# Hymba-style encoder trunk on one core: GLA scores of both directions by turns on row halves, output products in two column halves

## The chip, the cores and the metric

The kernel runs on one core of a Trainium2 chip. The metric is the device time of one execution in microseconds; the time before is the median of three runs.

## What is computed

Two layers of a bidirectional encoder over 1024 tokens of width 1024. Each layer adds to x an output projection of three head groups that share one input projection. The change touches two of them: the gated linear attention (GLA, 4 heads, key width 64, value width 96, one scan per direction) and the cross-attention into 256 memory tokens (4 heads of width 64). Cut to these:

```python
def _gla_chunked(q, k, v, g):
    b = jnp.cumsum(g, axis=-2)
    q_e = q * jnp.exp(b)
    k_e = k * jnp.exp(-b)
    a = jnp.where(incl, jnp.einsum('bhncd,bhnsd->bhncs', q_e, k_e), 0.0)
    o_intra = jnp.einsum('bhncs,bhnsv->bhncv', a, v)
    ...
    return o_intra + jnp.einsum('bhncd,bhndv->bhncv', q_e, s_prev)
...
    scores = jnp.einsum('bthd,bmhd->bhtm', q3, mk) * (XA_DH ** -0.5)
    p = jax.nn.softmax(scores, axis=-1)
    o3 = jnp.einsum('bhtm,bmhd->bthd', p, mv)
```

The GLA runs once forwards and once backwards and both are summed. The third group, a gated delta rule, is a serial recurrence over 16 chunks in both directions.

## The kernel before

Tokens stand in 8 tiles of 128. In each layer a first part normalises and transposes x and makes the dense projections (matmuls of 128x128 by 512 columns, in three passes of split fp32). Then `phase_mix` runs the serial chain of the delta rule (`chain`, matmuls that the trace shows as cp<-S,wq, R<-vn,kend, cp<-vn,qkt, pt<-kv,Mb and pt<-Mb,ke) and fills the time between its steps with other work: after each block of the chain, `filler` hands out units until their nominal nanoseconds reach a budget of 1200. What is left when the chain ends follows without it.

One kind of filler is the mixer (`mixes`), one tile of tokens after the other in the order `ORD`. For a tile it steps two generators:

- `xa_tile` has five units: softmax scores of two heads (x<-kh,xq and x<-kl,xq: four matmuls; then VectorE takes the maximum and ScalarE two exponentials); scores of the other two; transposes of the first two heads' exponentials (ident,pe), copied to pT; transposes of the other two; the value product (mv,pT: 128x128 by 64 columns, 4 heads by 2 halves of the memory).
- `gla_tile` has three units before: scores of one direction (x<-gqk or ga<-gqk: 64 rows, one row half of the array, by 128 columns, 4 heads), masked into As by a VectorE copy; scores of the other direction on the other row half, masked into the same As; then GpSimd multiplies As by `twice`, and TensorE forms the output product (gS,gqk and gv,As: 128x128 by 96 columns, 4 heads each).

Every mixer unit counts 700 nominal ns. All matmuls keep their program order, so a matmul that waits holds up all behind it, those of the chain as well. Other engines' instructions are placed by a scheduler. Four tiles of a layer are mixed while the chain runs and four afterwards, between the matmuls of the output projection (mm<-wo,oh and mm<-wo,ol; `out_tile`).

While the chain runs, PSUM tags ga, gb and tr stand for the tag x, which has two banks; gb becomes mm (two banks) in the middle of it. After the chain ga, gb and tr have two banks each. The tiles gqk, gv, gS (loads of the GLA) and xq have one buffer each, so a load waits until the tile's last reader is done.

An fp32 matmul is two records in the trace: the four score matmuls of a direction show as x8.

Of the kernel before, what the change touches and what calls it, by code (L numbers as in the profile page):

```python
# [17 lines left out]
P = 128  # L18
# [3 lines left out]
NT = 8  # L22
# [20 lines left out]
DC0 = 0  # L43
CUT = 30
MIX0 = 5
MIXN = 18
GAP0 = 4
GU = (4, 6)
TRN = 4
# [6 lines left out]
ORD = (4, 3, 5, 2, 6, 1, 7, 0)  # L56


class Kern:
# [768 lines left out]
    def filler(self, l, xin, xout, GP, closeGP):  # L828
# [28 lines left out]
        done = units = 0  # L857
        busy = True
        while busy:
            if units < 24:  # L860
                next(mixer)
                units += 1
                yield 700
            while busy and done < units * left // MIXN:

                if self.h0_done:
                    next(wout, None)
                busy = next(self.dense, None) is not None
                done += 1
                if busy:  # L870
                    yield 1290
# [2 lines left out]
        self.alias["gb"] = "mm"  # L874
        while self.wo[0][KT - 1] is None:
            next(wout)
            if units < 24:
                next(mixer)
                units += 1
                yield 700  # L880
        self.closeW()
        self.open_out(l)
        for _ in range(units, 24):
            next(wout, None)
            next(mixer)
            yield 700
# [10 lines left out]
        for i in range(NT + 1):  # L897
            g = None
            if i:
                t = ORD[i - 1]  # L900
                if i < NT:
                    x = self.OB.tile([P, D], F32, tag="xr", name="xr", bufs=1)
                else:
                    x = self.OX.tile([P, D], F32, tag="big", name="xr", bufs=2)
# [5 lines left out]
                for u, _ in enumerate(self.out_tile(self.OB, t, x, xout, then)):  # L910
# [6 lines left out]
                    if g is None and ready(i):  # L917
                        g = self.gate_tile(self.OG, ORD[i])
# [4 lines left out]
            while i < NT and g is None:  # L923
                if ready(i):
                    g = self.gate_tile(self.OG, ORD[i])
# [24 lines left out]
    def open_mix(self):  # L950
        self.OX, self.closeOX = self.pool("OX", side=self.sb)
        self.xa_setup(self.OX)
        self.gla_setup(self.OX)
        self.om, self.loaded = {}, {}
        self.mixed = 0
        self.mix_load(ORD[0])

    def open_out(self, l):
        self.OG, self.closeOG = self.pool("OG", side=self.sb)
# [3 lines left out]
            self.fw = self.OB.tile([P, D], F32, name="fw")  # L963
            self.nc.sync.dma_start(self.fw, self.a["final_norm_w"].to_broadcast([P, D]))

    def mix_load(self, t):
        self.loaded[t] = self.xa_load(self.OX, t), self.gla_load(self.OX, t)

    def mixes(self):

        for i, t in enumerate(ORD):
            o = self.om[t] = self.OX.tile([P, 640], F32, tag="o", name="o", bufs=3)
            xl, gl = self.loaded.pop(t)
            x = self.xa_tile(self.OX, xl, o[:, 384:640])
            g = self.gla_tile(self.OX, gl, o[:, 0:384])
            for j, u in enumerate((x, g, x, g, x, x, g, x)):
                next(u, None)
                if j == 6 and i + 1 < NT:
                    self.mix_load(ORD[i + 1])
                if j == 7:  # L980
                    self.mixed = i + 1
                yield

# [372 lines left out]
    def gla_tile(self, G, loaded, o):  # L1356

        qk, vt, S = loaded
        A = G.tile([P, 4, P], F32, tag="As", name="As", bufs=2)
        for d in range(2):  # L1360
            pa = self.ps("ga", [P, 4, P])
            r = slice(d * 64, d * 64 + 64)
            for h in range(4):
                self.mat(pa[:, h, :], qk[r, h, 1, :], qk[r, h, 0, :], start=True, stop=True)
            self.nc.vector.copy_predicated(A, self.mask[d].unsqueeze(1).to_broadcast([P, 4, P]), pa)  # L1365
            yield
        self.ptt(A, A, self.twice.unsqueeze(1).to_broadcast([P, 4, P]), ALU.mult)
        po = self.ps("gb", [P, 4, HD])
        for h in range(4):
            self.mat(po[:, h, :], qk[:, h, 0, :], S[:, h, :], start=True, stop=False)  # L1370
            self.mat(po[:, h, :], A[:, h, :], vt[:, h, :], start=False, stop=True)
        self.act(o.rearrange("p (h d) -> p h d", h=4), po)
        yield

# [74 lines left out]
    def xa_tile(self, XP, xq, o):  # L1449

        nc = self.nc
        mv = self.mv
        sc = 64 ** -0.5
        pe = XP.tile([P, 4, MEM], F32, tag="big", name="pe", bufs=2)
        sm = XP.tile([P, 4], F32, tag="xsm", name="xsm", bufs=2)
        mx = XP.tile([P, 4], F32, tag="xmx", name="xmx", bufs=2)

        for hh in range(2):
            psc = self.ps("ga", [P, 2, MEM])
            hs = slice(hh * 2, hh * 2 + 2)  # L1460
            for pr in range(2):
                i = hh * 2 + pr
                self.mat(psc[:, pr, :], xq[:, i, :], self.kh[:, i, :], start=True, stop=False)
                self.mat(psc[:, pr, :], xq[:, i, :], self.kl[:, i, :], start=False, stop=True)
            nc.vector.tensor_reduce(mx[:, hs], psc, op=ALU.max, axis=AX.X)
            nc.vector.tensor_scalar(mx[:, hs], mx[:, hs], -sc, None, op0=ALU.mult)
            for pr in range(2):
                i = hh * 2 + pr
                self.act(pe[:, i, :], psc[:, pr, :], AF.Exp, scale=sc, bias=mx[:, i:i + 1],
                         accum_out=sm[:, i:i + 1])  # L1470
            yield
        nc.vector.reciprocal(sm, sm)
        pT = XP.tile([P, 4, 2, P], F32, tag="big", name="pT", bufs=2)
        for g in range(2):
            ps = self.ps("gb", [P, 4, P])
            for j in range(4):
                i, m = g * 2 + j // 2, j % 2
                self.tpose(ps[:, j, :], pe[:, i, m * 128:m * 128 + 128], self.ident)
            self.evac(pT[:, g * 2:g * 2 + 2].rearrange("p a b c -> p (a b) c"), ps)
            yield  # L1480
        po = self.ps("gb", [P, 4, 64])
        for i in range(4):
            hd = (i % 2) * 2 + i // 2
            for m in range(2):
                self.mat(po[:, i, :], pT[:, i, m, :], mv[:, m, hd * 64:hd * 64 + 64],
                         start=m == 0, stop=m == 1)

        self.tt(o.rearrange("p (q h d) -> p h q d", q=2, h=2),
                po.rearrange("p (h q) d -> p h q d", h=2),
                sm.rearrange("p (h q) -> p h q", h=2).unsqueeze(3).to_broadcast([P, 2, 2, 64]), ALU.mult)  # L1490
        yield
# [164 lines left out]
```

## Time and profile before

| | us |
|---|---|
| runs | 1433.19, 1434.46 (median), 1443.61 |
| profiled execution, its own time | 1429.31 |
| its span, first to last instruction | 1427.6 |
| TensorE busy in the span | 1298.7 |
| VectorE, ScalarE, GpSimd busy | 841.6, 633.7, 566.9 |

Busy time of TensorE counts each matmul until its modelled end, so neighbours overlap; what a matmul costs the engine is read from start to start. In the first layer the mixer's matmuls lie from 495 to 675 us, in the second from 1202 to 1392 us; the chain ends near 590 and 1303 us.

### The profile page before, as it was taken

The numbers are of one execution on the slowest core, as the hardware profiler recorded it, in microseconds if no ns is written. First come the engines' busy times: TensorE is split into PE (matmuls) and PEld (weight loads), VectorE is DVE, ScalarE is ACT, GpSimd is POOL, SyncE is SP. The second block draws the span as 40 slices with busy tenths as digits, with TensorE's granted clock in tenths as the row PEclk, the third lists the DMA queues.
The fourth block names the chain that finished last, engine by engine and source line by source line (L and its number), as shares of the span: only waits on it lengthen the run. The fifth ranks groups of instructions, "written<-read, shape, count | busy, mean of one in ns | idle before, by whom it ended". The sixth has DMA issues, their size and how long they took to land. (4 is left out here: it accounts for less than half of the span.)

```text
span 1427.6 us, 23239 instructions
## 1 busy us (share of the span) xinstructions
PE 1298.7 (91%) x8970; PEld 1089.7 (76%) x8970; DVE 841.6 (59%) x1267; ACT 633.7 (44%) x1269; POOL 566.9 (40%) x597
## 2 busy tenths in 40 slices
PE   6998799898899989999899978987978999999998
PEld 5986588676687778888798757865857877888886
DVE  5346864595678455445362677536947874545553
ACT  5344654254655443223252455513355554433332
POOL 3035435494434345212310544354953344442111
PEclk9999999998999999999999999998989999989999
DMA  7251325733787654253543413266346875622432
GB/s 224 64 117 45 103 61 158 250 115 97 198 225 202 186 179 120 78 156 114 186 158 79 98 30 104 84 179 217 89 122 184 242 220 157 211 86 78 155 100 104
DMA packets 247855, 198.94 MB, mean 139 GB/s; under 512 B 68032, under 2 KB 215936, under 8 KB 247744
## 3 DMA queue, kind: packets, MB, share of 16 engines
q1 hardware_dynamic: 245584, 189.59, 46.1%
q10 hardware_dynamic: 2016, 7.34, 1.3%
q8 instruction: 71, 1.16, 0.3%
q0 software_dynamic: 144, 0.52, 0.1%
q14 instruction: 40, 0.33, 0.1%
HBM read 138.82 MB, written 58.59 MB: 138 GB/s over the span
## 5 line engine op out<-in xcount | busy, mean ns | idle before, releaser
L97 PE MATMUL mm<-Hh,wh 128*128 128x512 f32 x736 | 311.5, 423 | 36.5 <-ACT acc L83 19.6
L97 PE MATMUL mm<-Hh,wl 128*128 128x512 f32 x736 | 295.2, 401 | 0.0
L97 PE MATMUL mm<-Hl,wh 128*128 128x512 f32 x736 | 295.2, 401 | 0.0
L89 POOL TENSOR_TENSOR wl<-wr,wh 128x1024 fp32r<-128x1024 f32 x46 | 119.1, 2588 | 205.2 <-ACT wh L83 182.8
L97 PEld LDWEIGHTS mm<-Hh,wh 128*128 128x128 f32 x736 | 143.1, 194 | 71.0 <-ACT acc L83 22.9
L534 DVE SCALAR_TENSOR_TENSOR acc<-pad,convw,acc 128x1024 f32<-128x1024 f32 x72 | 141.5, 1966 | 67.9 <-ACT acc L83 53.1
L97 PE MATMUL mm<-wo,oh 128*128 128x512 f32 x512 | 167.5, 408 | 0.4 <-ACT oh L83 0.4
L97 PEld LDWEIGHTS mm<-Hh,wl 128*128 128x128 f32 x736 | 143.2, 195 | 32.2
L97 PEld LDWEIGHTS mm<-Hl,wh 128*128 128x128 f32 x736 | 144.1, 196 | 25.9
L97 PEld LDWEIGHTS mm<-wo,oh 128*128 128x128 f32 x512 | 89.8, 189 | 18.6 <-ACT oh L83 0.8
L97 PE MATMUL mm<-wo,ol 128*128 128x512 f32 x256 | 101.2, 395 | 0.6 <-POOL ol L89 0.6
L89 POOL TENSOR_TENSOR acc<-acc,pad 128x1024 f32<-128x1024 f32 x18 | 45.6, 2532 | 109.8 <-ACT pad L83 109.8
L89 POOL TENSOR_TENSOR S<-S,dec 96x384 f32<-96x384 f32 x56 | 52.6, 939 | 84.8 <-DVE S L86 54.8
L83 ACT ACTIVATE wh<-wr 128x1024 fp32r<-128x1024 f32 x46 | 48.4, 1053 | 75.7 <-PE mm L97 60.7
L89 POOL TENSOR_TENSOR ol<-z,oh 128x512 fp32r<-128x512 f32 x32 | 40.9, 1281 | 93.6 <-ACT oh L83 89.7
L97 PEld LDWEIGHTS cp<-S,wq 96*128 96x128 f32 x480 | 64.9, 204 | 16.3 <-ACT vn L83 4.9
L97 PE MATMUL cp<-S,wq 96*128 96x96 f32 x480 | 68.3, 289 | 9.3 <-ACT vn L83 3.6
L89 POOL TENSOR_TENSOR sp<-sp,sg 128x512 f32<-128x512 f32 x32 | 44.0, 1376 | 44.1 <-ACT sg L83 33.3
L97 PEld LDWEIGHTS mm<-wo,ol 128*128 128x128 f32 x256 | 48.1, 188 | 12.5 <-POOL ol L89 1.1
L97 PEld LDWEIGHTS R<-vn,kend 64*96 64x96 f32 x448 | 43.3, 165 | 16.9 <-issue 8.1
L89 POOL TENSOR_TENSOR row<-row,qT 96x1024 f32<-96x1024 f32 x16 | 38.0, 2385 | 45.2 <-DMA row<-row_d 29.4
L89 POOL TENSOR_TENSOR As<-As,twice 128x512 f32<-128x512 f32 x16 | 20.4, 1276 | 86.9 <-DVE As L1365 46.7
(313 smaller groups left out, 2746.3 us busy)
## 6 DMA issues: line engine op xcount, KB each, us to landing
wr<-in_w_in_dram SPq DMA_DIRECT2D x46, 512.0 KB, 4.1
kv<-kv_d SPq DMA_DIRECT2D x32, 384.0 KB, 3.9
zT<-sp SPq DMA_DIRECT2D x32, 256.0 KB, 3.0
ge_d<-qe SPq DMA_DIRECT2D x32, 256.0 KB, 3.7
wor<-in_w_out_dram SPq DMA_DIRECT2D x16, 512.0 KB, 4.3
gqk<-ge_d SPq DMA_DIRECT2D x16, 512.0 KB, 4.1
z<-zT SPq DMA_DIRECT2D x16, 512.0 KB, 4.5
row<-row_d SPq DMA_DIRECT2D x16, 384.0 KB, 6.6
```

Source lines behind the costliest of these rows:

```text
L83: return self.nc.scalar.activation(out, in_, func, **kw)
L89: return self.nc.gpsimd.tensor_tensor(out, a, b, op=op)
L97: return self.pin(self.nc.tensor.matmul(*args, **kw))
L534: nc.vector.scalar_tensor_tensor(acc, pad[:, j:j + T], self.convw[:, f, j:j + 1], acc, op0=ALU.mult, op1=ALU.add)
```

## The change

The GLA scores of both directions become one unit: each has a PSUM bank of its own, and the matmuls alternate between the directions, which means between row halves of the array. The output product and the value product write the same results, but each matmul is split into two with 64 stationary columns, for PSUM partitions 0 to 63 and 64 to 127, by turns. A tile then has seven units instead of eight, in a new order: both softmax scores, both transposes, GLA scores, value product, GLA output. The load of xq is issued after the second unit, that of the GLA's tiles after the last. The counts that spread the first three tiles over the dense work change with it (24 to 21 units, 18 to 16).

```diff
-MIXN = 18
+MIXU = 21
+MIXN = 16
...
-            if units < 24:
+            if units < MIXU:
...
-            xl, gl = self.loaded.pop(t)
-            x = self.xa_tile(self.OX, xl, o[:, 384:640])
-            g = self.gla_tile(self.OX, gl, o[:, 0:384])
-            for j, u in enumerate((x, g, x, g, x, x, g, x)):
+            x = self.xa_tile(self.OX, self.loaded["x"], o[:, 384:640])
+            g = self.gla_tile(self.OX, self.loaded["g"], o[:, 0:384])
+            for j, u in enumerate((x, x, x, x, g, x, g)):
                 next(u, None)
-                if j == 6 and i + 1 < NT:
-                    self.mix_load(ORD[i + 1])
-                if j == 7:
+                if j == 1 and i + 1 < NT:
+                    self.loaded["x"] = self.xa_load(self.OX, ORD[i + 1])
+                if j == 6:
+                    if i + 1 < NT:
+                        self.loaded["g"] = self.gla_load(self.OX, ORD[i + 1])
                     self.mixed = i + 1
...
+        pa = [self.ps("ga", [P, 4, P]) for _ in range(2)]
+
+        for h in range(4):
+            for d in range(2):
+                r = slice(d * 64, d * 64 + 64)
+                self.mat(pa[d][:, h, :], qk[r, h, 1, :], qk[r, h, 0, :], start=True, stop=True)
         for d in range(2):
-            pa = self.ps("ga", [P, 4, P])
-            r = slice(d * 64, d * 64 + 64)
-            for h in range(4):
-                self.mat(pa[:, h, :], qk[r, h, 1, :], qk[r, h, 0, :], start=True, stop=True)
-            self.nc.vector.copy_predicated(A, self.mask[d].unsqueeze(1).to_broadcast([P, 4, P]), pa)
-            yield
+            self.nc.vector.copy_predicated(A, self.mask[d].unsqueeze(1).to_broadcast([P, 4, P]), pa[d])
         self.ptt(A, A, self.twice.unsqueeze(1).to_broadcast([P, 4, P]), ALU.mult)
+        yield
         po = self.ps("gb", [P, 4, HD])
+
+        cs = [slice(c * 64, c * 64 + 64) for c in range(2)]
         for h in range(4):
-            self.mat(po[:, h, :], qk[:, h, 0, :], S[:, h, :], start=True, stop=False)
-            self.mat(po[:, h, :], A[:, h, :], vt[:, h, :], start=False, stop=True)
+            for c in cs:
+                self.mat(po[c, h, :], qk[:, h, 0, c], S[:, h, :], start=True, stop=False)
+            for c in cs:
+                self.mat(po[c, h, :], A[:, h, c], vt[:, h, :], start=False, stop=True)
...
-                self.mat(po[:, i, :], pT[:, i, m, :], mv[:, m, hd * 64:hd * 64 + 64],
-                         start=m == 0, stop=m == 1)
+
+                for c in (slice(0, 64), slice(64, 128)):
+                    self.mat(po[c, i, :], pT[:, i, m, c], mv[:, m, hd * 64:hd * 64 + 64],
+                             start=m == 0, stop=m == 1)
```

What this does to TensorE's queue is shown at three places. In these rows a count is of matmuls (two records each). First, the end of the second tile of the first layer, during the chain. Before:

```order
L97 MATMUL cp<-S_4713,wq 128x96 x4
L97 MATMUL pt<-Mb_3166,ke 96x128 x4
L97 MATMUL x<-gqk 128x128 x4
L100 MATMUL mm<-ident,pe 128x128 x8
L97 MATMUL mm<-gS,gqk 128x96
L97 MATMUL mm<-gv,As 128x96
```

And with the change:

```order
L98 MATMUL cp<-S_4734,wq 128x96 x4
L98 MATMUL pt<-Mb_3166,ke 96x128 x4
L98 MATMUL x<-gqk 128x128 x8
L98 MATMUL mm<-mv,pT 64x64 x16
L98 MATMUL mm<-gS,gqk 64x96 x2
L98 MATMUL mm<-gv,As 64x96 x2
```

Between the last scores and the first gv,As stand now the value product's 16 half matmuls, where eight transposes stood; and only the second direction's scores came so late before. Second, the fourth tile of the first layer, with the change:

```order
L98 MATMUL x<-kh,xq 128x256
L98 MATMUL x<-kl,xq 128x256
L98 MATMUL x<-kh,xq 128x256
L98 MATMUL x<-kl,xq 128x256
L101 MATMUL mm<-ident,pe 128x128 x8
L98 MATMUL mm<-wo_4698,oh 128x512 x2
```

Before, these scores were followed by other work:

```order
L97 MATMUL x<-kh,xq 128x256
L97 MATMUL x<-kl,xq 128x256
L97 MATMUL x<-kh,xq 128x256
L97 MATMUL x<-kl,xq 128x256
L97 MATMUL R<-vn,kend 96x96 x4
L97 MATMUL x<-gqk 128x128 x4
L97 MATMUL mm<-wo_4677,oh 128x512 x2
```

So the transposes of the second pair of heads now come directly behind that pair's scores. Third, after the chain, where a tile's units lie between output matmuls; with the change:

```order
L98 MATMUL ga<-gqk 128x128 x8
L101 MATMUL tr<-ident,o 128x128 x3
L101 MATMUL tr<-ident,oa_3161 128x128
L98 MATMUL mm<-wo_5049,oh 128x512 x2
L98 MATMUL mm<-wo_5049,ol 128x512
L98 MATMUL mm<-wo_5076,oh 128x512 x2
L98 MATMUL mm<-wo_5076,ol 128x512
L98 MATMUL gb<-mv,pT 64x64 x16
L98 MATMUL mm<-wo_5093,oh 128x512 x2
```

Here the scores, the value product and the output product keep six output matmuls (two steps of wo) between each other, as before.

## Rows read from the trace of the kernel before

**Rows 1.** The page: span, and busy time of the engines.
```profile
span 1427.6 us, 23239 instructions
...
PE 1298.7 (91%) x8970; PEld 1089.7 (76%) x8970; DVE 841.6 (59%) x1267; ACT 633.7 (44%) x1269; POOL 566.9 (40%) x597
```

**Rows 2.** Windows: length, busy us (x instructions) of PE, PEld, DVE, ACT, POOL, granted clock, DMA.
```profile
494.90:580.00 85.10, 80.15 (x674) 71.60 (x672) 47.65 (x90) 36.61 (x89) 43.48 (x45) 0.98 0.47 138
...
592.00:672.00 80.00, 80.00 (x482) 67.83 (x481) 42.21 (x88) 25.76 (x69) 16.50 (x13) 1.00 0.41 124
...
1242.30:1259.30 17.00, 17.00 (x88) 16.16 (x89) 8.59 (x18) 5.65 (x16) 4.89 (x5) 0.50 0.29 89
1214.00:1300.00 86.00, 81.52 (x633) 73.55 (x628) 42.99 (x81) 33.72 (x78) 34.46 (x36) 0.90 0.44 133
```

**Rows 3.** Timeline of PE after the chain: start us, length us, instruction, records.
```profile
594.72 0.40 PE L97 MATMUL mm<-wo,ol 128*128 128x512 f32 x1
595.05 1.16 PE L97 MATMUL ga<-gqk 64*128 64x128 f32 x8
596.13 0.73 PE L97 MATMUL mm<-wo,oh 128*128 128x512 f32 x2
...
606.32 0.35 PE L97 MATMUL gb<-gS,gqk 128*128 128x96 f32 x2
...
608.07 0.38 PE L100 MATMUL tr<-ident,oa 128*128 128x128 f32 x2
...
609.91 1.89 PE L97 MATMUL gb<-mv,pT 128*128 128x64 f32 x16
611.61 0.71 PE L97 MATMUL mm<-wo,oh 128*128 128x512 f32 x2
```

**Rows 4.** Timeline of PE, one of 16 groups of column-half matmuls, 64 wide.
```profile
241.81 0.40 PE L97 MATMUL mm<-Hl,wh 128*128 128x512 f32 x1
242.04 0.40 PE L97 MATMUL mm<-Hh,wl 128*128 128x512 f32 x1
242.37 0.34 PE L97 MATMUL cp<-kT 96*64 96x64 f32 x4
...
243.45 0.50 PE L97 MATMUL mm<-Hh,wh 128*128 128x512 f32 x1
```

**Rows 5.** Timeline of PE, one of 16 groups of column-half matmuls, 96 wide.
```profile
413.79 0.88 PE L97 MATMUL x<-gv,kt 128*64 128x96 f32 x16
414.60 0.50 PE L97 MATMUL mm<-Hh,wh 128*128 128x512 f32 x1
```

**Rows 6.** Timeline of PE, GLA scores and R on different row halves.
```profile
521.89 0.32 PE L97 MATMUL R<-vn,kend 64*96 64x96 f32 x1
521.99 0.27 PE L97 MATMUL x<-gqk 64*128 64x128 f32 x1
522.05 0.24 PE L97 MATMUL R<-vn,kend 64*96 64x96 f32 x1
522.11 0.27 PE L97 MATMUL x<-gqk 64*128 64x128 f32 x1
```

**Rows 7.** Groups by form, DVE, ACT and POOL: busy us, mean ns, idle before.
```profile
L1465 DVE TENSOR_REDUCE xmx<-x 128x2 f32<-128x512 f32 x16 | 11.0, 690 | 8.5 <-PE x L97 8.3
L1365 DVE COPY_PREDICATED As<-mB,x 128x512 f32<-128x512 int32 x8 | 5.9, 733 | 1.6 <-PE x L97 1.6
...
L83 ACT ACTIVATE pe<-x,xmx 128x256 f32<-128x256 f32 x32 | 14.9, 469 | 25.5 <-DVE xmx L1466 25.5
L83 ACT ACTIVATE pT<-x 128x512 f32<-128x512 f32 x6 | 3.5, 591 | 1.7 <-PE x L100 1.6
...
L89 POOL TENSOR_TENSOR As<-As,twice 128x512 f32<-128x512 f32 x16 | 20.4, 1276 | 86.9 <-DVE As L1365 46.7 <-DVE xsm L1472 40.2
```

**Rows 8.** Groups of PE from 494 to 580 us with the longest idle time before them.
```profile
L97 PE MATMUL cp<-S,wq 96*128 96x96 f32 x104 | 14.1, 278 | 1.9 <-ACT vn L83 1.8
...
L100 PE MATMUL x<-ident,pe 128*128 128x128 f32 x16 | 3.0, 320 | 1.4 <-ACT pe L83 1.4
```

More of the change, by code (lines that the diff above doesn't have):

```diff
@@ L876, in filler @@
             next(wout)
-            if units < 24:
+            if units < MIXU:
                 next(mixer)
@@ L882, in filler @@
         self.open_out(l)
-        for _ in range(units, 24):
+        for _ in range(units, MIXU):
             next(wout, None)
@@ L955, in open_mix @@
         self.mixed = 0
-        self.mix_load(ORD[0])
+        self.loaded["x"], self.loaded["g"] = self.xa_load(self.OX, ORD[0]), self.gla_load(self.OX, ORD[0])
     def open_out(self, l):
@@ L964, in open_out @@
             self.nc.sync.dma_start(self.fw, self.a["final_norm_w"].to_broadcast([P, D]))
-    def mix_load(self, t):
-        self.loaded[t] = self.xa_load(self.OX, t), self.gla_load(self.OX, t)
     def mixes(self):
```

## The prediction

> **What bounds the kernel now.** I read the page first: TensorE is busy for 1298.7 of 1427.6 us, the next engine for 841.6 [rows 1]. Then the windows, since the change lives in two stretches of each layer. After the chain, from 592 to 672 us, TensorE is busy for all 80.00 us at full clock, VectorE for 42.21, ScalarE for 25.76 [rows 2]: there every nanosecond taken from its queue should come off the time. While the chain runs and tiles are mixed, from 494.9 to 580 us, it is busy for 80.15 of 85.10 us, so 4.95 us are waits; the same stretch of the second layer has 81.52 of 86.00, 4.48 us of waits [rows 2]. The busiest other engine there has 47.65 us. So TensorE's queue, with its waits, is the time, and I count in starts along that queue.
>
> One more thing is to be seen in the windows: the granted clock. From 1242.3 to 1259.3 us it is 0.50 (1.2 instead of 2.4 GHz) with TensorE busy throughout, and 0.90 over the whole second stretch; in the first layer it is 0.98 over the stretch [rows 2], which is 0.02 x 85.1 x 2 = 3.4 us at half clock.
>
> **The change part by part.** A lone matmul record of the dense kind follows the one before after 0.23 us (241.81 to 242.04) [rows 4]; what a unit adds to such a stream is its cost.
>
> *Scores.* Eight records of one direction start at 595.05, the next output matmul at 596.13: 1.08 us, and the way in took 0.33 instead of 0.23 us [rows 3]. So 1.18 us a unit, two units a tile, 2.36 us. Can two row halves run at once with full columns? No row shows this very unit, but one place does nearly: scores and R on the other row half ran into each other. Scores start at 521.99 and 522.11, 0.12 us apart, no more than the 1.08 / 8 = 0.135 of an undisturbed unit, with records of R at 521.89 and 522.05 between them [rows 6]. Neither stream gave way. So 16 records by turns should take what eight take: 1.18 us. Bounds: 0 saved if the halves don't overlap and only one way in and out (0.2 us) goes, 1.18 if they do. I take 1.18, by rows 6.
>
> *Value product.* Now 16 records from 609.91 to 611.61, 1.70 us [rows 3]. That is 0.106 us each for 64 columns, while the 96-wide ones of the output product take 1.75 / 16 = 0.109; the width is not what is paid. After: 32 records of 64 stationary columns, 64 wide, on two column halves. The rows of the kT group are just that (32 records, 96 rows instead of 128): from 242.37 to 243.45 1.08 us, and 0.10 more on the way in (242.04 to 242.37 instead of 0.23) [rows 4]: 1.18 us. Saved 0.52.
>
> *Output product.* Now from 606.32 to 608.07, 1.75 us [rows 3]. After: 32 records, 96 wide, in column halves. Sixteen such records take from 413.79 to 414.60, 0.81 us with the way out [rows 5]. Twice that, 1.62, is the most; the least is 0.81 and eight pairs more at 0.08 (0.81 less some 0.2 for the ends, over eight pairs), 1.45. I take 1.5, and 0.1 for the way in as above: 1.6. Saved 0.15 (0.03 to 0.2).
>
> Sum for a tile: 1.18 + 0.52 + 0.15 = 1.85 us; 16 tiles, 29.6 us. Half of it, 14.8 us, lies after the chain, where the order shows six output matmuls (6 x 0.23 = 1.4 us) between any two units, and VectorE and ScalarE have half their time free. There I expect no new wait: As is ready 2 x 0.73 + 1.28 = 2.7 us, with handing over some 3.0, after the scores [rows 7], and six output matmuls (1.4), the value product (1.2) and another six (1.4) stand before it is read.
>
> *Waits during the chain.* Here the new order takes cover away. All of what follows is for four tiles of a layer, in the order shown.
> First tile: both banks of x are needed by the scores at once, and the second is freed by the copy of the second transposes (0.59 us, some 0.8 with handing over) [rows 7], which stand directly before: 0.8 us.
> Second tile: As is ready some 3.0 us after the scores, and only the value product (1.18) stands between: 1.9 us, where the one-direction unit waited less, since one masked copy was long done.
> Third tile: transposes of the first heads need a maximum (0.69), a scaling, two exponentials of 0.47 with the read of their sums [rows 7], some 2.2 us; a chain step and the second scores cover about 1.4: 0.8 us. Then As again with one chain step more before it: 0.9 us.
> Fourth tile: the second transposes directly behind their scores: 2.2 less the first transposes' 0.45, 1.75 us.
> Together 6.1 us a layer. What goes: the wait of 1.4 us on exponentials [rows 8] and the rest that hangs on the GLA's late loads, some 3 us of the 4.95 together; the chain's own 1.9 us on vn [rows 8] stays. Queued behind each of these waits are the chain's next steps, so they count in full. Net 3.1 us a layer, 6.2 in all; bounds: 0, if the chain would wait there anyway, and 12, if nothing of the old waits goes.
>
> *Clock.* 17.0 and 3.4 us at half clock now cost up to 10.2 us. The trace can't show what the new order does to them. Bounds: all of it is won (10.2), or as much comes again (-10). The value products and scores become denser, which should shorten the long spell, but the waits of some 2 us are longer than any now. I take half of what stands: 5 us won.
> The Trainium skill, in "TensorE: Matmul & The Clock Gate", Part 1, has the clock fall after idle time and rise after busy time; in the long spell the trace shows it staying low while TensorE counts as busy throughout [rows 2]. By that rule alone the long spell would not last, and its 8 us would be no term at all.
>
> The rest costs nothing: the loads of xq and of the GLA tiles come earlier against their readers (four units of cover instead of two), and SP's queue holds the same transfers; VectorE and ScalarE do the same operations. Two banks for the scores cost what is counted above.
>
> Sum against the profiled execution: 1429.3 - 29.6 + 6.2 - 5 = 1400.9. The runs' median is 5.2 us above that execution, so I forecast **1406 us**. A measurement of this kernel can tell about 1% from no change.
>
> **Rivals.**
> *A: the chain's stretch gives nothing.* Waits and lost cover eat the 14.8 us of the eight tiles there, the clock stays as it is: 1434.5 - 14.8 = 1420. For it: every unit there now hangs on another engine's answer; against it: the first tile's 1.4 us wait goes for sure.
> *B: the clock stays up* and the waits hide in the chain's own: 1434.5 - 29.6 - 8 = 1397. For it: the spell in the second layer has no counterpart at the same place of the first [rows 2], so a small shift can remove it.
> *C: row halves take turns.* The change then doesn't do what it says for the scores; 1.0 us a tile, 16 us, are lost of the gain, and the clock's share with it: 1434.5 - 13.6 + 6.2 = 1427. Against it stand rows 6.
> *D: column halves don't overlap, slower.* Each product then has 32 records one after another. A half record alone costs between 0.05, half of what a whole one does now, and 0.106 [rows 3]; at 0.08, 32 are 2.6 us instead of 1.70 and 1.75, so 1.75 us more a tile against the scores' 1.18 less: 0.57 x 16 = 9 more, with the waits 1434.5 + 9 + 6 = 1450. It decides from 0.13 us a pair on ((5.81 - 1.18 - 0.6) over 32 pairs). Rows 4 and 5 are against it (1.08 / 16 = 0.07 and 0.81 / 8 = 0.10 a pair).
> The Trainium skill has such a rule in "TensorE: Matmul & The Clock Gate", Part 3 (The mechanism): weight loads overlap running matmuls only when the row group differs, which column halves don't; the trace disagrees, with 16 records in 0.81 us [rows 5].
> *E: half clock spreads* over the chain's stretches, behind the new waits. From some 50 us more at 1.2 GHz than now the gain is gone; 80 us more give 1434.5 - 23.4 + 40 = 1451. Against it: after the chain the clock is 1.00 throughout [rows 2], so it could only be the chain's two stretches of 86 us.
>
> **How the numbers follow.** Forecast (1400 to 1413) 0.52, B 0.2, A 0.15, C 0.05, D 0.03, E 0.05. The range runs from 1392, B with all 10 us of the clock and no wait added (1434.5 - 29.6 - 10 = 1395) less 3 for the units' own bounds, to 1424, above A; C, D and E lie outside. Faster by over 1% (under 1420) takes the forecast, B and 0.1 of A: 0.82; within 1%: the rest of A, C and 0.02 of E, 0.12; slower: D and the rest of E, 0.06.
>
> **What would show it.** After the chain the time between two tiles' GLA scores falls by 1.85 us; the scores' 16 records take about as long as eight did, the value product 1.2 us, the output product 1.6. TensorE's rows during the chain show idle time on As, pe and pT, about 8 us a layer. I am wrong if score records of both directions don't start in pairs, if those idle times pass 12 us a layer, or if the windows show more half clock than the 20 us of now.

## The result and the profile after

The changed kernel takes 1425.0 us (median), the kernel before 1434.2: ratio 0.9935, 95% interval 0.991 to 0.996. The forecast was 1406.0 with a range of 1392 to 1424. So the change is worth some 9 us, not 28, and the time lies just outside the range, on the side of too little gain.

The page after (span and busy time, as [rows 1]):

```profile
span 1427.6 us, 24281 instructions
...
PE 1289.7 (90%) x9482; PEld 1068.1 (75%) x9482; DVE 843.9 (59%) x1267; ACT 631.4 (44%) x1269; POOL 568.6 (40%) x597
```

The two profiled executions happen to have the same span (before's was 4.9 us faster than its median, after's 4.4 us slower), so where the time went must be read inside. Only the stretch from the first softmax-score matmul to the last output matmul of each layer has changed. These are the windows over it, before and after (columns as in [rows 2]), with the two longest half-clock spells of after beneath:

```profile
494.91:708.48 213.57, 207.58 (x1388) 177.47 (x1387) 103.47 (x200) 71.53 (x177) 72.78 (x89) 0.99 0.45 136
1201.73:1420.28 218.55, 213.49 (x1387) 183.62 (x1387) 111.03 (x206) 80.20 (x199) 65.65 (x62) 0.96 0.39 123
```

```profile
495.43:708.61 213.18, 200.05 (x1643) 165.65 (x1643) 105.48 (x200) 70.14 (x176) 73.37 (x86) 0.96 0.45 135
546.40:560.00 13.60, 13.60 (x76) 12.37 (x72) 3.05 (x5) 3.80 (x8) 6.61 (x8) 0.50 0.49 131
1206.07:1420.23 214.16, 202.13 (x1643) 166.21 (x1643) 111.06 (x206) 78.88 (x199) 63.80 (x60) 0.95 0.41 125
1256.30:1273.40 17.10, 16.34 (x102) 15.05 (x103) 3.11 (x7) 3.90 (x8) 7.31 (x9) 0.50 0.37 105
```

What to see: TensorE's busy time falls from 207.58 + 213.49 = 421.07 to 402.18 us, 18.9 us less; but the length falls only from 432.12 to 427.34, because its idle time (length less busy) rises from 11.05 to 25.16 us. And the granted clock falls from 0.99 to 0.96 in the first layer and from 0.96 to 0.95 in the second: the spells at half clock in these stretches add up to 20.5 us before and 37.5 us after. Outside the stretches the two executions differ too, with 102.0 us at half clock before and 125.6 after; how much of it stands there differs from one execution to the next (101.5 in e8, the same kernel again). So the stretches account for 4.8 us between two single executions, and the rest of the 9 us between the medians has no account here.

Cut at the last matmul of the chain, the same stretches read, before and then after:

```profile
494.91:590.25 95.34, 90.39 (x743) 80.14 (x742) 50.94 (x95) 37.71 (x91) 45.77 (x47) 0.98 0.44 128
1201.73:1302.88 101.15, 96.67 (x743) 86.47 (x742) 51.24 (x95) 37.87 (x91) 42.89 (x44) 0.92 0.42 126
```

```profile
495.43:598.36 102.93, 92.14 (x887) 78.86 (x886) 54.05 (x98) 37.92 (x92) 47.33 (x48) 0.93 0.43 124
1206.07:1310.86 104.79, 94.62 (x887) 81.57 (x886) 53.93 (x97) 39.65 (x96) 42.40 (x43) 0.90 0.42 123
```

Beside the chain idle time rises from 4.95 and 4.48 to 10.8 and 10.2 us, and the part becomes 7.6 and 3.6 us longer, of which some 3 us are output and score matmuls that stood behind the chain before. Behind the chain each layer is 8.0 us shorter (118.23 to 110.25 and 117.40 to 109.37). What the change gains, it gains behind the chain.

The timeline of TensorE behind the chain (as [rows 3]):

```profile
605.69 0.40 PE L98 MATMUL mm<-wo,ol 128*128 128x512 f32 x1
606.02 1.16 PE L98 MATMUL ga<-gqk 64*128 64x128 f32 x16
607.11 0.55 PE L101 MATMUL tr<-ident,o 128*128 128x128 f32 x3
...
608.77 0.40 PE L98 MATMUL mm<-wo,ol 128*128 128x512 f32 x1
609.10 1.15 PE L98 MATMUL gb<-mv,pT 128*64 128x64 f32 x32
610.18 0.72 PE L98 MATMUL mm<-wo,oh 128*128 128x512 f32 x2
...
611.77 0.39 PE L98 MATMUL gb<-gS,gqk 128*64 128x96 f32 x4
...
613.24 0.44 PE L101 MATMUL tr<-ident,oa 128*128 128x128 f32 x2
...
624.06 0.71 PE L98 MATMUL ga<-gqk 64*128 64x128 f32 x7
```

Sixteen score records go from 606.02 to 607.11, 1.09 us, as long as eight did. The value product goes from 609.10 to 610.18, 1.08 us, with 0.33 us from the record before it; the output product from 611.77 to 613.24, 1.47 us. The next tile's scores start at 624.06, 18.04 us after 606.02, where 20.0 us stood before. In the second layer a tile takes 18.3 to 18.4 us (19.9 before, apart from one of 20.9).

The waits of TensorE from 490 to 598 us (in total, times, longest), as [rows 8]:

```profile
PE mm L98 <- POOL As L90: 5.4, 2, 3.0
PE cp L98 <- ACT vn L84: 2.4, 3, 1.3
PE mm L101 <- ACT pe L84: 1.7, 3, 1.1
PE x L98 <- DVE pT L115: 0.7, 1, 0.7
PE x L101 <- ACT pe L84: 0.4, 1, 0.4
```

The largest is the wait for As, 2.46 us in the second tile and 2.97 in the third; before, it was 0.4 us once in this layer. Why it is so long can be read from the third tile, TensorE first, then VectorE, then GpSimd:

```profile
538.60 1.16 PE L98 MATMUL x<-gqk 64*128 64x128 f32 x16
539.70 1.15 PE L98 MATMUL mm<-mv,pT 128*64 128x64 f32 x32
540.78 1.13 PE L98 MATMUL cp<-S,wq 96*128 96x96 f32 x8
541.84 0.39 PE L98 MATMUL mm<-gS,gqk 128*64 128x96 f32 x4
545.19 0.39 PE L98 MATMUL mm<-gv,As 128*64 128x96 f32 x4 [2.97 <-POOL As L90]
...
539.94 0.73 DVE L1366 COPY_PREDICATED As<-mF,x 128x512 f32<-128x512 int32 x1
540.64 0.85 DVE L87 TENSOR_TENSOR o<-o,oss 128x384 f32<-128x384 f32 x1
541.41 1.35 DVE L87 TENSOR_TENSOR oa<-oa,oss 128x384 f32<-128x384 f32 x1
542.68 0.41 DVE L87 TENSOR_TENSOR o<-o,oss 128x256 f32<-128x256 f32 x1
543.02 0.71 DVE L1366 COPY_PREDICATED As<-mB,x 128x512 f32<-128x512 int32 x1
...
543.88 1.26 POOL L90 TENSOR_TENSOR As<-As,twice 128x512 f32<-128x512 f32 x1 [1.53 <-DVE As L1366]
```

Both directions' scores are done by 539.76 (538.60 + 1.16), and the first masked copy starts 0.2 us later. But the second starts only at 543.02: three normalisations of another tile (gate_tile) stand between the two on VectorE. As is ready 5.4 us after the scores, and the value product and a chain step cover 2.1 of these. The Trainium skill, "TensorE: Matmul & The Clock Gate", Part 1 (Architectural detail), has VectorE and ScalarE take their queues strictly in order; the trace agrees, the second copy had its input and stood 2.4 us behind the three. Right behind this wait, at 546.40, the clock falls to 0.50, and it stays there for 13.60 us though TensorE is busy in every one of them. In the second layer it falls at 1256.3, still inside the third tile's wait of 2.97 us (1254.09 to 1257.06).

### The profile page after: what moved, and what is told of

It reads as the page before. It is cut to its first block, busy times and chain, and to the rows that moved or that the text cites. A ratio compares the mean times of both kernels' runs of the same rounds, so it can differ in the third digit from the quotient of the medians.

```text
span 1427.6 us, 24281 instructions
## 1 busy us (share of the span) xinstructions
PE 1289.7 (90%) x9482; PEld 1068.1 (75%) x9482; DVE 843.9 (59%) x1267; ACT 631.4 (44%) x1269; POOL 568.6 (40%) x597
## 5 line engine op out<-in xcount | busy, mean ns | idle before, releaser
L98 PE MATMUL mm<-Hl,wh 128*128 128x512 f32 x736 | 298.4, 405 | 0.0
L98 PE MATMUL mm<-Hh,wl 128*128 128x512 f32 x736 | 298.3, 405 | 0.0
L98 PE MATMUL mm<-wo,ol 128*128 128x512 f32 x256 | 101.5, 396 | 0.0
L98 PEld LDWEIGHTS cp<-S,wq 96*128 96x128 f32 x480 | 65.7, 206 | 18.3 <-ACT vn L84 6.1
L98 PEld LDWEIGHTS R<-vn,kend 64*96 64x96 f32 x448 | 46.2, 174 | 19.0 <-issue 8.9
L98 PE MATMUL R<-vn,kend 64*96 64x96 f32 x448 | 55.4, 268 | 1.8 <-DVE S L87 1.7
```

Of the source, the lines that this page charges most:

```text
L98: return self.pin(self.nc.tensor.matmul(*args, **kw))
```

## The experiments

Theory 1: TensorE sets the time in the whole stretch; what the new order makes it wait (for As above all), and the half clock that sets in behind such waits, ate the gain. Theory 2 (rival A's sum, with another reason than its own): beside the chain the chain's own latency sets the pace, so whatever TensorE saves there is lost anyway. Theory 3, for the clock alone: it falls for another reason than idle time.

The table has all runs. Length and idle are sums over both layers' stretches, from the windows as above (first softmax-score matmul to last output matmul); half clock is what the granted clock shows at 0.50 in them. Each of these three is from one profiled execution. The runs were made in several rounds on several chips, and each ratio is to before in the same round, whose median was between 1425.6 and 1434.2 us; so runs are compared by their ratios, and not by their times.

| run | time us | ratio to before (95%) | length | idle | half clock |
|---|---|---|---|---|---|
| before | 1434.2 | 1 | 432.1 | 11.1 | 20.5 |
| after | 1425.0 | 0.9935 (0.991 to 0.996) | 427.3 | 25.2 | 37.5 |
| e8 after again | 1423.8 | 0.9938 (0.991 to 0.9966) | 430.0 | 26.6 | 41.0 |
| e1 columns only | 1426.1 | 0.9995 (0.9964 to 1.0027) | 429.5 | 16.5 | 30.7 |
| e2 order only | 1444.5 | 1.0117 (1.0081 to 1.0152) | 452.4 | 18.5 | 61.4 |
| e6 whole products | 1439.6 | 1.0053 (1.002 to 1.0085) | 442.7 | 21.0 | 51.2 |
| e3 chain step between | 1414.9 | 0.9909 (0.9877 to 0.9942) | 414.9 | 20.3 | 20.5 |
| e4 filler in the wait | 1408.5 | 0.9886 (0.9842 to 0.9931) | 415.5 | 19.6 | 6.8 |
| e5 filler behind it | 1426.6 | 0.998 (0.9945 to 1.0016) | 425.1 | 25.5 | 20.5 |
| e7 multiply on VectorE | 1422.3 | 0.9947 (0.9913 to 0.9982) | 421.0 | 24.2 | 23.9 |
| e9 scores one unit earlier | 1408.5 | 0.9875 (0.9824 to 0.9926) | 416.2 | 22.4 | 17.1 |
| e12 the same again | 1412.8 | 0.9892 (0.9848 to 0.9935) | 417.0 | 21.4 | 23.9 |
| e10 scores two units earlier | 1442.5 | 1.0121 (1.0065 to 1.0178) | 443.2 | 38.2 | 41.0 |
| e11 one unit earlier, chain steps between | 1405.4 | 0.9835 (0.9783 to 0.9887) | 411.7 | 15.8 | 27.3 |

**e1: the column halves alone.** The order and scores of before, with

```diff
+        cs = [slice(c * 64, c * 64 + 64) for c in range(2)]
         for h in range(4):
-            self.mat(po[:, h, :], qk[:, h, 0, :], S[:, h, :], start=True, stop=False)
-            self.mat(po[:, h, :], A[:, h, :], vt[:, h, :], start=False, stop=True)
+            for c in cs:
+                self.mat(po[c, h, :], qk[:, h, 0, c], S[:, h, :], start=True, stop=False)
+            for c in cs:
+                self.mat(po[c, h, :], A[:, h, c], vt[:, h, :], start=False, stop=True)
```

and the same in the value product.

> The order of before; only the GLA output product and the value product are split into two column halves. Both theories give it the shorter groups: 32 value matmuls from 1.70 to about 1.2 us a tile, output product from 1.75 to about 1.6, so 0.67 us a tile. Theory 1 (PE's waits and half-clock spells in the new order ate the gain): no new waits here, PE idle between 490 and 720 us stays at the 9.3 us of before, and all sixteen tiles keep their gain: 16 x 0.67 = 10.7 us, about 1423.5 (ratio 0.9925). Theory 2 (beside the norm chain the chain's own latency sets the pace, whatever PE saves there): only the eight tiles behind the two chains count: 5.4 us, about 1429 (0.996), with PE idle beside the chain up by 2 to 3 us a layer.

Measured: 0.9995, no change. Behind the chain a tile takes 19.4 instead of 20.0 us in the first layer, as worked out. Over the stretches busy time falls, but idle time rises from 11.1 to 16.5 us (the load of gqk, waited for 0.5 and 0.8 us before, is now waited for 1.3 and 2.9), and the half clock from 20.5 to 30.7. Neither theory had this: a forecast gain of 10.7 us in matmuls came to nothing without any new order. Waits, for a load among others, and the clock account for it in this one execution; no run here takes them apart.

**e2: the order alone, and e6: the order with scores by turns.** e6 is after with both products whole (the diff of e1 the other way round); e2 besides has

```diff
-        for h in range(4):
-            for d in range(2):
+        for d in range(2):
+            for h in range(4):
```

> The order of after (both score directions in one unit, four softmax units ahead of it, seven units a tile), but the eight score matmuls one direction after the other and both products whole: no matmul form is changed. Theory 1: it carries the new waits alone, some 7 us of PE idle a layer more than before, and a few us of half clock, against one switch of matmul form less a tile (about 0.2 us x 16 = 3): about 1445 to 1452 (1.008 to 1.012). Theory 2 (the chain sets the pace beside it in either order): the order is nearly free, about 1432 (0.998).

> The kernel after with both products whole again: only the order and the scores by turns on row halves are left. Behind the chains, where no wait differs, the period of a tile tells the prices apart: 20.0 us before, 19.2 to 19.5 with the new order alone (e2), 19.4 with the column halves alone (e1), 18.0 to 18.4 with all. If the row halves overlap, 18.6 to 18.8 here; if they take turns on the array, 19.2 to 19.5 as in e2. Beside the chains theory 1 (idle before As, then half clock) expects the waits of after and spells of at least its length: 1428 to 1440 in all; theory 2 (the chain's pace) expects after's 1425 plus 5 for the eight tiles behind the chains: 1430.

Measured: e2 1.0117, slower by 1.2%. That is theory 1's time, but in part by luck: idle time rose by 3.7 us a layer and not by 7, and 61.4 us at half clock, three times that of before and not a few us more, made up for it. e6 1.0053, where theory 2's 1430 would be 0.997: the row halves are worth 0.64% of the time, 9 us, on top of the order (the two intervals just touch); behind the chain a tile takes 18.7 us in the first layer, against 19.2 in e2 and 18.0 in after. That the row halves overlap is plain from the scores themselves, sixteen records one direction after the other in e2 and by turns in e6:

```profile
619.97 1.71 PE L98 MATMUL ga<-gqk 64*128 64x128 f32 x16
621.61 0.55 PE L101 MATMUL tr<-ident,o 128*128 128x128 f32 x3
```

```profile
615.03 1.16 PE L98 MATMUL ga<-gqk 64*128 64x128 f32 x16
616.12 0.55 PE L101 MATMUL tr<-ident,o 128*128 128x128 f32 x3
```

They take 1.64 us in e2 and 1.09 in e6, so by turns they save 0.55 us a tile; the other 0.6 of the 1.18 us forecast comes from making one unit of two, without any overlap, where the prediction had given that 0.2. After against e6 gives the column halves 1.2%, some 16 us, in this order, where e1 gave them nothing in the old one. Theory 2 falls for the order: it isn't free beside the chain.

The busy time of TensorE tells the matmuls' own share. In the runs with after's matmuls (after, e3, e7 to e12) it goes from 393.8 us with 17.1 us at half clock (e9) to 403.4 with 41.0 (e8): 0.4 us for each us at half clock (a straight line through all eight gives 0.45). Taking that off at 0.4, I estimate 413 us for before, 409 for e2, 401 for e6 and 387 for after: the order saves 4, the row halves 8, the column halves 14, together 26 us; 29.6 were forecast. For e1 the same gives 401, 12 us less than before.

**e3: a chain step between the units.**

```diff
-                yield
+                yield 1300 if j in (4, 5) else 700
```

with `yield c` in the three places where the mixing schedule passed on 700.

> The kernel after, but the units with the GLA scores and the value product are entered in the mixing schedule at 1300 instead of 700 ns, so that a step of the norm chain stands between the scores and the value product and between that and the GLA output product. Nothing that is computed changes. Theory 1: PE finds work while As is multiplied and copied; its idle before the GLA output product beside the chain (2.46, 2.97, and 4.7 in two in the second layer) falls to under 1 us a layer, about 10 us, and the half-clock spell behind the longest goes: about 1412 (0.985). Theory 2: what PE wins there it waits for at the chain's next step, about 1425 (0.9935).

Measured: 0.9909, less than theory 1's 0.985, with an interval that overlaps after's. The wait for As is gone beside both chains (one of 1.7 us behind the first chain stays). Waits for S, exps and pT of 1 to 2 us took part of its place, as theory 2 says, but the sum is less (20.3 us), the half clock is back at 20.5, and the stretches are 12.4 us shorter than after's.

**e4: filler in the wait; e5: filler behind it.** e4 issues the value product three times, e5 the GLA output product twice, both in the second and third tile of a layer alone:

```diff
-        for i in range(4):
+        for _ in range(3 if self.mixed in (1, 2) else 1):
+            for i in range(4):
```

> The kernel after, but in the second and third tile of each layer the value product is issued three times with the same result, so that about 2 us more of matmuls stand before the GLA output product that waits for As; it does more work than after, and its time is read so. Theory 1 with a clock that falls behind the idle: the idle before the GLA output product falls by about 2 us in each of these tiles, the added work lies in it and costs nothing, and the 13.6 us spell at half clock right behind the 2.97 us wait in the first layer goes, which is 5 to 7 us back: 1418 to 1425. Theory 3 (the clock falls for another reason than this idle): the idle is filled but the spell stays, 1425 or a little more (0.994).

> The kernel after, but in the second and third tile of each layer the GLA output product is issued twice with the same result: 1.5 us more of matmuls in the same tiles as in e4, but behind the wait for As and not in it. If the clock falls because PE stands idle for As: the waits stay (2.46 and 2.97 us in the first layer, 1.75 and 2.97 in the second), the half-clock spells that begin behind the 2.97 us waits stay too (13.6 and 17.1 us), and the added 6 us are paid in full: about 1431 (0.997). If e4 was faster because more matmuls run there, wherever they stand: the spells go here as well, about 1412 (0.989).

Measured: e4, whose value product takes 2.95 instead of 1.08 us in four tiles and which so does some 7.5 us more work than after, is no slower but faster by its ratio: 0.9886 against 0.9935 (the intervals just overlap), at the fast end of theory 1's range (1418 would be 0.9887). e5, with 6 us more work in the same tiles, has 0.998, some 6 us above after and e8, as if paid in full; but the intervals overlap, and in the medians of its own round it is 2.8 us above e8. The waits of TensorE in e4 from 490 to 590 us:

```profile
PE cp L98 <- ACT vn L84: 2.5, 3, 1.4
PE mm L98 <- POOL As L90: 2.3, 2, 1.2
...
```

and in e5 from 491 to 596 us:

```profile
PE mm L98 <- POOL As L90: 4.7, 2, 3.0
PE cp L98 <- ACT vn L84: 2.6, 3, 1.5
...
```

The window of e5 right behind its wait of 2.97 us:

```profile
545.60:549.00 3.40, 3.40 (x42) 3.17 (x37) 0.00 (x0) 0.38 (x1) 0.00 (x0) 0.50 0.02 5
```

In e4 the wait in the third tile is 1.12 us and no spell follows it; its windows over the two chains show a clock of 0.98 both times:

```profile
489.70:588.50 98.80, 90.68 (x1014) 77.85 (x1013) 55.90 (x97) 37.98 (x92) 47.72 (x48) 0.98 0.45 129
...
1192.90:1290.60 97.70, 90.68 (x1014) 78.01 (x1013) 54.33 (x97) 39.47 (x96) 44.74 (x46) 0.98 0.44 132
```

In e5 the wait stands, and so does a spell behind it in both layers, but of 3.4 and 6.8 us instead of 13.6 and 17.1. e5's profiled execution was also the fastest of its runs (1418.7 us against a median of 1426.6), so its spells need not be the usual ones.

Two runs are few, but the fourteen profiles of the table settle theory 3 together. In their stretches stand 54 spells at 1.2 GHz, and every one begins inside a wait of TensorE of 0.8 us or more, or at most 2.2 us behind its end. All 13 waits of over 2.8 us have such a spell, and 41 of the 139 waits from 0.8 us up to that. So idle time goes ahead of every fall of the clock, and theory 3 falls. How long a spell lasts doesn't follow from its wait: the 17 us of before begin behind 0.80 us for the load of gqk,

```profile
1242.15 1.99 PE L97 MATMUL x<-gqk 64*128 64x128 f32 x8 [0.80 <-DMA gqk<-ge_d]
```

while behind after's wait of 2.46 us for As none stands.

**e7: the multiplication on VectorE.**

```diff
-        self.ptt(A, A, self.twice.unsqueeze(1).to_broadcast([P, 4, P]), ALU.mult)
+        self.tt(A, A, self.twice.unsqueeze(1).to_broadcast([P, 4, P]), ALU.mult)
```

> The kernel after, but the multiplication of As by its mask (1.26 us on GpSimd) is done on VectorE, where a pass over a 128x512 tile takes 0.7 us. Nothing else changes. Theory 1 (the wait for As is what costs, itself and by the clock): the wait is 0.6 us shorter in every tile, 2.46 and 2.97 become about 1.9 and 2.4; 3 us less idle in all and shorter half-clock spells: 1415 to 1422. Theory 2 (the chain sets the pace there): no change, 1425; it could even lose where VectorE's copies for the softmax queue behind the multiplication.

Measured: 0.9947, no difference from after. In the second tile the wait falls to 1.2 us, in the third it stays at 2.9: there the three normalisations between the copies set it, and the multiplication queued behind two more instructions on VectorE. My expectation took GpSimd's 1.26 us for the price; where it mattered, the price was VectorE's queue.

**e8: after again.**

> The kernel after once more, unchanged, on the same chip as the three others: how far its half-clock spells repeat from one profiled execution to the next. Theory 1 (they begin behind the waits of the order) expects spells at the same places, behind the waits for As near 545 and 1257 us, of 10 to 17 us; if they were chance, they stand elsewhere or are gone. Time about 1425 (0.9935).

Measured: 0.9938, the same. Spells of 17.1 us from 546.6 and of 13.7 us from 1256.6, at waits of 2.97 us for As, as in after (546.4 and 1256.3). Their places belong to the order; their lengths changed sides. Smaller ones stand elsewhere than in after.

**e9 and e12: GLA scores one unit earlier; e10: two units earlier.**

```diff
-            for j, u in enumerate((x, x, x, x, g, x, g)):
+            for j, u in enumerate((x, x, x, g, x, x, g)):
```

and (x, x, g, x, x, x, g) in e10.

> The kernel after, but the GLA scores stand between the two units of softmax transposes and no more behind both: the second four transposes and the chain steps of one unit more lie between the scores and the GLA output product. Nothing else changes; scores and transposes are matmuls of one form, so no switch is added. Theory 1 (the wait for As is late because VectorE's queue and GpSimd come between): with one unit more of cover the waits for As in the second and third tile (2.46 and 2.97 us) fall to under 1 us, the spells at half clock behind them go or shorten to 3.4 to 7 us, the waits for the softmax exps stay: 1408 to 1415 (0.985). Theory 2 (the chain's pace): 1424 as after.

> The kernel of e9 once more, unchanged, beside e11 on one chip: whether its gain repeats, and whether its one long wait (5.21 us for gqk in the second layer) and its 13.7 us spell ahead of the mixing belong to the kernel or to one execution. Theory 1: no wait for As again, 0.9875 again (about 1408 where before takes 1426). A wait for gqk of several us that stands in the same place would be the price of the earlier scores.

> The kernel after, but the GLA scores stand ahead of the softmax transposes, so that they also fill the time in which PE waits for the exps (0.3 to 1.1 us a tile), and As has both transposes, the value product and two units of chain steps to be ready; VectorE's two copies into As stand next to each other in every tile of the chain. Theory 1: no wait for As is left, the waits for the exps fall by half, spells as in e4 (3.4 us): 1402 to 1410 (0.981). Against it: the load of gqk (4.0 us) has two units less to land, and the scores may wait for it behind the chains; 0.5 to 1 us a tile would give back 8 to 16 us. Theory 2: 1424.

Measured: 0.9875 and 0.9892 for e9's kernel (each interval still overlaps the edge of after's), 1.0121 for e10. The waits of e9 from 490 to 598 us:

```profile
PE cp L98 <- ACT vn L84: 1.7, 3, 0.6
PE mm L98 <- DVE pT L115: 1.7, 2, 1.5
PE x L98 <- ACT pe L84: 1.5, 1, 1.5
...
```

and from its timeline the two copies into As of the third tile:

```profile
539.59 0.73 DVE L1366 COPY_PREDICATED As<-mF,x 128x512 f32<-128x512 int32 x1 [0.41 <-PE x L98]
540.42 0.74 DVE L1366 COPY_PREDICATED As<-mB,x 128x512 f32<-128x512 int32 x1
```

The copies stand next to each other, no product waits for As any more, and the first layer's stretch is 202.4 us, 10.8 less than after's. The second layer gains nothing (213.8): the scores' second bank is held there by softmax scores whose exps come late (their maximum stands on VectorE behind a vn that waits 4.0 us for GpSimd): 5.21 us, and again 5.19 us in e12. In e10 this happens more often. Its waits from 594 to 670 us, behind the first chain, and from 1312 to 1390, behind the second:

```profile
PE ga L98 <- ACT pe L84: 2.7, 4, 1.6
...
PE ga L98 <- ACT pe L84: 7.8, 8, 1.6
```

I had expected the load of gqk to be waited for; it is, but for 1.9 us a layer. The price is the two banks: the GLA scores of both directions need both, and directly behind the softmax scores both are still read by the exps, 5.4 us beside the first chain and 9.0 beside the second. Another 4.8 us in the second layer are one wait of the chain's for u from ScalarE, which no run here explains.

**e11: e9 with chain steps at the other two waits.** `yield 1300 if j in (1, 4) else 700` on top of e9.

> The kernel of e9 (GLA scores between the two units of softmax transposes), and besides the second softmax-score unit and the second transpose unit are entered in the mixing schedule at 1300 instead of 700 ns, so that a chain step stands behind the scores, where PE waits for the exps (0.8 us a tile in e9), and one between the transposes and the value product, where it waits for the copy of pT (1.1 and 1.5 us). Theory 1 (each of these waits costs itself and may start a half-clock spell): some 2 us less idle a layer than in e9, shorter spells, chains that end 5 us earlier as in e3: 1400 to 1406 (0.983). Theory 2 (the chain's pace): PE waits at the chain's next steps instead, and the time is that of e9, 1408 (0.9875).

Measured: 0.9835, 1405.4 us, the fastest of all. Its windows over the two stretches:

```profile
494.28:700.47 206.19, 198.59 (x1643) 166.05 (x1643) 103.71 (x200) 69.97 (x176) 72.65 (x86) 0.96 0.47 140
1200.31:1405.86 205.55, 197.39 (x1644) 163.22 (x1643) 111.67 (x206) 78.35 (x199) 66.01 (x62) 0.98 0.43 131
```

7.60 and 8.16 us of idle time (after: 13.13 and 12.03), and the 5.2 us wait of the second layer is gone. TensorE does the work of after in stretches 15.6 us shorter. The profiled execution was the slowest of its runs. e11's interval overlaps those of e4, e9 and e12, so that it beats before and after is shown, and that it beats these three isn't. Theory 2 falls for good: with the same matmuls and the same chain, five orders (after, e3, e9, e10, e11) differ by up to 31 us in these stretches, and up to the chain's last matmul alone e11 takes 190.6 us over both layers, where before takes 196.5 and after 207.7.

## Why the prediction was wrong

The forecast for these stretches was -29.6 for the matmuls, +6.2 for waits, -5 for the clock: -28.4. The profile has -26 (estimated above), +14.1, and +17.1 us of half clock at 0.4, some +7: -5, and the length of the stretches fell by 4.8. (The medians of the runs fell by 9; the stretches are one execution of each kernel.) Two terms failed: the waits, because As was taken to be ready 3.0 us after its scores, and the clock, which was booked as a gain apart from the waits. Point by point:

- **Matmul prices: right.** Scores by turns 1.09 us and the way in (1.18 forecast), value product 1.08 and 0.10 (1.18), output product 1.47 us from 611.77 to 613.24 and 0.10 (1.6). The period behind the chain fell by 2.0 us in the first layer and 1.6 in the second (1.85). Rivals C and D, that the halves don't overlap, are out: e2's scores against e6's show it for the rows, and the two products' shorter times, in e1 as in after, for the columns. C's price of 1.0 us a tile was too high, it is 0.55.
- **No new wait behind the chain: nearly right.** One wait of 1.7 us for As in the first layer, two of 1.5 us together for exps in the second; in all, idle time there rose by 1.3 us a layer.
- **Waits during the chain: the mechanism right, the size of one term wrong.** As, exps and pT were named, at 6.1 us a layer, with some 3 of old waits gone. TensorE's idle time beside the chain rose by 5.8 and 5.7 us instead of 3.1. The waits for exps and pT came out at 2.8 us in the first layer, where 3.35 were forecast; those for As at 5.4 us in the first layer and 4.7 in the second, where 1.9 + 0.9 = 2.8 were. What failed is the step "As is ready some 3.0 us after the scores": it added up two copies and the multiplication as if their queues were empty. In the second tile VectorE's copy waits for a vn of the chain, and As is ready 3.7 us after the last score; in the third three normalisations stand between the copies, for 2.4 us (some 1.0 of them by the slowness described at the end), and it is 5.4 us. e7, where a shorter multiplication leaves the third tile's wait at 2.9 us, agrees that it is VectorE's queue, and in e9, with one unit more of cover and the copies side by side, As is no wait any more.
- **Clock: the step that cost most.** It was taken as 5 us won, from bounds of 10 either way; it cost about 7, which with the 5 is 12 of the 23 us between forecast and stretches. Half of what stood was a choice with no row behind it. The waits and the clock were booked as two separate terms. They belong together: each of the long spells of after and e8 begins in or right behind a wait for As of 2.97 us, and e4, which fills most of that wait with useless work, takes both away. The prediction said that the new waits "are longer than any now", and then let the denser matmuls weigh more.
- **The rule on the clock.** The Trainium skill, "TensorE: Matmul & The Clock Gate", Part 1, has the clock fall after idle time and rise after busy time. The fall agrees with all 54 spells here. That busy time soon brings the clock back doesn't show: 13.60 us at 0.50 with TensorE busy for all 13.60.
- **Rival A** (1420, the chain's stretch gives nothing) had the sum nearly right and the reason half: waits and lost cover ate the gain there, as it said, but the clock did not stay as it was; **rival E**, that half clock spreads behind the new waits, was the mechanism, at 17 us more instead of its 80.
- **What would make it wrong** named one sign that came, more than 20 us of half clock (37.5). The other, idle times during the chain past 12 us a layer, did not come: they are 10.8 and 10.2 us, and on As, pe and pT alone 8.2 in the first layer, where "about 8" was expected.

What stays open is what sets how long a spell lasts (3.4 to 6.8 us at the same wait in e5, 13.6 to 17.1 in after and e8) and which of the shorter waits has one; and whether an order with few waits in e1's manner would give the column halves their worth without the new order.

## What to carry to other kernels

Before an operation's cover is cut down, write out the queue of every engine on the way back to its reader, as the scheduler will leave it: a copy that "takes 0.7 us" was 2.4 us late because three instructions of another tile stood between it and its twin. Book a wait of a few us on TensorE together with the half clock that may follow it (here 0.4 us for every us of a spell of up to 17), and not as two terms that may cancel. Here a wait was removed by an order that puts work into it; moving the multiplication to a faster engine did nothing, and moving the work too early ran into banks that were still being read.

## What the runs showed that was not expected

- More work made the kernel no slower, and faster by its ratio: some 7.5 us of repeated matmuls in waits of 2 to 3 us took 0.5% off the time (e4 against after, with intervals that just overlap), with 31 us less at half clock in the profiles.
- The clock can stay at its lower level for 13.6 to 17.1 us with TensorE busy almost throughout (16.34 of 17.10 us in the longest spell of after, 13.60 of 13.60 in the other).
- Shorter matmuls alone (e1) had more half clock than before, 30.7 against 20.5 us in one execution each, and no gain.
- VectorE's multiplication of oa took 1.35 us at 541.41, where the same form has a median of 0.55 us; GpSimd ran two passes over oa of 2.27 us from 540.08 beside it. Over all profiles of the table, the 26 of these multiplications that start while a GpSimd TENSOR_TENSOR is running take 1.18 to 1.64 us and end 0.42 us after it; the other 198 take about 0.55, the 16 beside which one starts later among them. In before the three normalisations take 1.4 us (547.95 to 549.32), so I estimate that about 1.0 of the 2.4 us that they held up the second copy comes from this. No run tried it apart.
